# Two attention heads at a time, one per half of TensorE's array and of the partitions

## The chip, the cores and the metric

One core of one Trainium2 chip runs the whole program in one launch. The metric is the device time of an execution in microseconds (us), median over executions. Two rows of the profile with the same name and shape can be passes of one f32 matmul: an f32 matmul is recorded as two.

## The reference

Two transformer blocks at batch 1, 256 tokens (two tiles of 128), width 1024, everything in float32, each block with two layers. In the first block a layer is: a mixer (an LRU, "fox" = causal attention with a forget gate in 8 heads of 64, "ret" = retention in 4 heads of 64), cross attention to a memory (4 heads of 256), and a SwiGLU ffn of 2816. In the second block a layer is: an ffn, a mixer of three branches (NSA with 8 query heads over 2 key heads in a compressed, a selected and a window branch; "sb", stick-breaking attention in 4 heads; "swa", sliding-window attention in 4 query heads over 2 key heads, with sinks), and another ffn. At 256 tokens the selected and the window branch are full causal attention.

```
fox:  softmax(q k^T / 8 + c_q - c_k, causal) v       8 heads
ret:  (q k^T / 8 * decay) v                          4 heads
sb:   w = exp(z - suffix sums of softplus(z)), w v   4 heads
swa:  softmax over 128 keys back, with a sink, v     4 heads
nsa:  g0*compressed + g1*softmax(..)v_slc + g2*softmax(..)v_win   8 heads x 2
```

## The kernel before

**Projections.** All large products run in three passes (high by high, high by low, low by high) with weights that arrive in 1 MB chunks (`Weights._load`, three raw buffers, on SP's queue). ScalarE rounds a chunk's half to the high part (`whi`), VectorE subtracts for the low part (`wlo`); up to six such pieces (`NPIECE`) are ready ahead. One piece of 2 x 512 columns feeds 12 matmuls of 512 columns. `nat_blocks` and `out_rows` loop over pieces and token tiles, with results in two PSUM tiles `acc`.

**Side work.** Attention and norms are Python generators in a list `sides`. After every half of a piece (six matmuls) `pump` steps those generators that are due by a planner (`Pace`): it adds up what each instruction should cost, e.g. on VectorE 0.065 us and 1.045 ns a column, on ScalarE 0.075 us and 0.86 ns a column and 0.09 us for a sum, for a matmul in f32 four passes of its columns at 2.4 GHz, for a DMA its bytes at 360 GB/s and 1.5 us. A generator yields until the planner's time of the data that it needs (`until`). The order so found is fixed in the program; on the chip each engine runs its queue in order. When main work asks for a k tile that isn't made (`need`), the side work is forced. Side work shares two PSUM tiles `aux`; attention's results gather in `o0` and `o1`.

**A head of attention before** (fox `scores`, `softmax_rows`, `transpose_probs`, `pv`; nsa and swa `scores`, `probs`, `turned`, `pv`): q and k lie with the 64 dimensions of two heads on the two halves of the partitions, so a head's score matmuls contract over 64 partitions. The causal 256 x 256 square is 384 columns: 128 for the first token tile, 256 for the second. VectorE adds bias or decay and finds the maximum, ScalarE takes the exponential and its sum. Two heads later the probabilities are turned (three transposes) and copied to SBUF; one head later three matmuls with the turned probabilities stationary and values moving (64 columns) give the result with tokens on partitions. After four heads a group is scaled by the reciprocal sums (and gates), turned with `to_T` (two transposes a token tile) and split into high and low for the next projection. `ret` has no softmax and `sb` two more triangular products; both have the same pattern of scores and `pv`.

**Padding.** `ffn(..., edge)` puts a tile of `edge` bytes a partition ahead of its activations `ahi`, `alo`; `edge` is 960 and 1472 in the first block's layers and 192, 256, 384, 160 in the second's four ffns, in the order in which they run. Tiles of few columns take 32 bytes a partition each in the pool `small`, which lies ahead of these; a tag there has four buffers.

Every engine instruction passes one helper line (150), so rows are told apart by tiles: out<-moving,stationary for a matmul.

Of the kernel before, what the change touches and what calls it, by code (L numbers as in the profile page):

```python
# [154 lines left out]
class Weights:  # L155
# [10 lines left out]
    def plan(self, ap, c0, c1, k0, k1, a_chunk, a_piece, split=True, gain=None):  # L166
        b = c1 - c0
        for k in range(k0, k1, a_chunk):
            a = min(a_chunk, k1 - k)
            ci = len(self.chunks)  # L170
            self.chunks.append((ap[k * P : (k + a) * P, c0:c1].rearrange("(a p) n -> p a n", p=P), a, b))
# [10 lines left out]
    def _load(self):  # L182
        if self.loaded >= len(self.chunks):
            return
        ap, a, b = self.chunks[self.loaded]
        t = self.raw_pool.tile([P, CHUNK], F32, tag="raw", name=f"raw{self.loaded}")
        v = t[:, : a * b].rearrange("p (a n) -> p a n", a=a)
        self.nc.sync.dma_start(v, ap)
        self.raw[self.loaded] = v
        self.loaded += 1  # L190
# [70 lines left out]
def tile_two_blocks(ctx, tc, I, out):  # L261
# [96 lines left out]
    def finish(gen):  # L358
        while any(i[0] is gen for i in sides):
            pump(force=True)  # L360

# [436 lines left out]
    def mixer1(l, T, cos, sin, next_maker):  # L798
        with nc.pool(tc, name=nm("mix1"), bufs=2) as mp:
# [16 lines left out]
            sums = one([P, 2, 8], "sums")  # L816
# [39 lines left out]
            def fox():  # L856
                st, nbs = {}, {}

                def load_nb(h):
                    nb = nbs[h] = mp.tile([P, 384], F32, tag="nb", name=nm("nb"))  # L860
# [4 lines left out]
                def scores(h):  # L865
                    b, r = h // 2, (h % 2) * 64
                    nb = nbs.pop(h)
                    ps = aux()
                    rs = slice(r, r + 64)
                    mm(ps[:, :P], fqT[rs, b, :P], fkT[rs, b, :P], start=True, stop=True)  # L870
                    mm(ps[:, P:384], fqT[rs, b, P:], fkT[rs, b, :], start=True, stop=True)
                    softmax_rows(st, h, ps, nb, sums[:, :, h])

                def softmax_rows(st, h, ps, nb, sum_):
                    sc = mp.tile([P, 384], F32, tag="sc", name=nm("sc"))
                    pr = sc
                    for t, (c0, c1) in enumerate(((0, P), (P, 384))):
                        ngm = sm(1, "ngm")
                        nc.vector.tensor_tensor_reduce(sc[:, c0:c1], ps[:, c0:c1], nb[:, c0:c1], -1.0, 1e38, ALU.add, ALU.min, ngm)
                        nc.scalar.activation(pr[:, c0:c1], sc[:, c0:c1], AF.Exp, bias=ngm, scale=-1.0, accum_out=sum_[:, t : t + 1])  # L880
                    st[h] = pr

                load_nb(0)
                yield
                for i in range(8 + 3):
                    if 0 <= i - 3 < 8:
                        h = i - 3
                        yield from until(st.pop(("T at", h)))
                        if h % 4 == 0:
                            ob = obank()  # L890
                            yield from until(nc.free[ob.tensor.name])
                        pv(ob[:, : 2 * S].rearrange("p (t n) -> p t n", t=2)[:, :, (h % 4) * 64 : (h % 4) * 64 + 64], st.pop(("T", h)),
                           fv[:, :, h * 64 : h * 64 + 64])
                        if h % 4 == 3:
                            g_ = h // 4
                            ri = mp.tile([P, 2, 4], F32, tag="ri", name=nm("ri"))
                            fo = mp.tile([P, 2, S], F32, tag="xs", name=nm("fo"))
                            nc.vector.reciprocal(ri, sums[:, :, 4 * g_ : 4 * g_ + 4])
                            nc.vector.tensor_tensor(fo.rearrange("p t (h d) -> p (t h) d", h=4), ob.rearrange("p (a d) -> p a d", d=64),
                                                    ri.rearrange("p t h -> p (t h)").unsqueeze(2).to_broadcast([P, 8, 64]), op=ALU.mult)  # L900
                            yield True
                            for t in (0, 1):
                                to_T(M, fo[:, t, :], t, 2 + 2 * g_, 2)
                                yield
                    if 0 <= i - 2 < 8:
                        yield from until(st.pop(("at", i - 2)))
                        st[("T", i - 2)] = transpose_probs(mp, st.pop(i - 2))
                        st["T at", i - 2] = nc.end
                        yield
                    if i < 8:  # L910
                        if i < 7:
                            load_nb(i + 1)
                        scores(i)
                        st["at", i] = nc.end
                        yield
# [84 lines left out]
            def ret():  # L1000
# [8 lines left out]
                decays = [load_decay(0)]  # L1009
                st = {}  # L1010
                for i in range(4 + 2):
                    if i < 3:
                        decays.append(load_decay(i + 1))
                    if i >= 2:
                        h = i - 2
                        if h == 0:
# [4 lines left out]
                        yield from until(st.pop(("at", h)))  # L1021
                        pv(ob.rearrange("p (t n) -> p t n", t=2)[:, :, h * 64 : h * 64 + 64], st.pop(h), rvg[:, :, h * 64 : h * 64 + 64])
                    if i < 4:
                        b, r = i // 2, (i % 2) * 64
                        rs = slice(r, r + 64)
                        ps = aux()

                        mm(ps[:, :P], rqkT[rs, 2 + b, :P], rqkT[rs, b, :P], start=True, stop=True)
                        mm(ps[:, P : 2 * P], rqkT[rs, 2 + b, P:], rqkT[rs, b, P:], start=True, stop=True)
                        mm(ps[:, 2 * P : 3 * P], rqkT[rs, 2 + b, :P], rqkT[rs, b, P:], start=True, stop=True)  # L1030
                        w = rot[:, i % 2, : 3 * P].rearrange("p (a q) -> p a q", a=3)
                        decay = decays.pop(0)
                        nc.vector.tensor_tensor(w[:, 0:2, :], ps[:, : 2 * P].rearrange("p (a q) -> p a q", a=2),
                                                decay[:, :P].unsqueeze(1).to_broadcast([P, 2, P]), op=ALU.mult)
                        nc.vector.tensor_tensor(w[:, 2, :], ps[:, 2 * P : 3 * P], decay[:, P:], op=ALU.mult)
                        st[i] = (w[:, 0, :], w[:, 2, :], w[:, 1, :])
                        st["at", i] = nc.end
# [40 lines left out]

    def transpose_probs(pool, pr):

        ps = aux()
        for c in range(3):
            turn(ps[:, c * P : (c + 1) * P], pr[:, c * P : (c + 1) * P], ident)
        w = pool.tile([P, 3, P], F32, tag="pt", name=nm("pt"))
        nc.scalar.copy(w, ps[:, :384].rearrange("p (c q) -> p c q", c=3))
        return (w[:, 0, :], w[:, 1, :], w[:, 2, :])
# [234 lines left out]
    def plan_mixer2(l):  # L1321
        w = I["w_in_2"][l]
        nat = lambda c0, n: W.plan(w, c0, c0 + n, 0, 8, 4 if n > 256 else 8, 2 if n > 256 else 4)
        up = lambda n, k: W.plan(I[f"w_up_{n}_2"][l], 0, D, 0, k, 2, 1)
# [13 lines left out]
        up("swa", 2)  # L1338
        gates(0)
        up("nsa", 4)  # L1340
        W.plan(I["w_out_2"][l], 0, D, 0, 8, 2, 1)

    def mixer2(l, T, next_maker):
        with nc.pool(tc, name=nm("mix2"), bufs=2) as mp:
# [11 lines left out]
            def tanh(out_, in_):  # L1356
# [3 lines left out]
            t2 = lambda: mp.tile([P, 512], F32, tag="t2", name=nm("t2"), bufs=2)  # L1360
            r3 = {"n": lambda: mp.tile([P, 384], F32, tag="rn", name=nm("rn"), bufs=5),
                  "s": lambda: mp.tile([P, 384], F32, tag="rs", name=nm("rs"), bufs=6)}
# [30 lines left out]

            def scores(q, k, rs):
                ps = aux()
                mm(ps[:, :P], q[rs, :P], k[rs, :P], start=True, stop=True)
                mm(ps[:, P:384], q[rs, P:], k[rs, :], start=True, stop=True)
                return ps

            def turned(ring, pr):  # L1400
                ps = aux()
                for c in range(3):
                    turn(ps[:, c * P : (c + 1) * P], pr[:, c * P : (c + 1) * P], ident)
                w = r3[ring]()
                nc.scalar.copy(w, ps[:, :384])
                return w[:, :P], w[:, P : 2 * P], w[:, 2 * P :]
# [20 lines left out]
            def swa():  # L1427
# [21 lines left out]
                ngm, sums = mp.tile([P, 8], F32, tag="wng", name=nm("wng")), mp.tile([P, 8], F32, tag="wsm", name=nm("wsm"))  # L1449
                bias = [load_bias(8), load_bias(9)]  # L1450
                st = {}
                for i in range(4 + 3):
# [15 lines left out]
                    if i < 4:  # L1468
                        if i < 2:
                            bias.append(load_bias(10 + i))  # L1470
# [550 lines left out]
```

## Time and profile before

| | |
|---|---|
| median of 3 executions | 2132.33 us (2129.34 to 2135.59) |
| the profiled execution | 2129.36 us |
| its span in the profile | 2127.4 us |
| TensorE, matmuls | busy 98% of the span |
| weight loads, VectorE, ScalarE, GpSimd | 83%, 59%, 53%, 5% |
| DMA | 179 GB/s over the span |
| granted clock of TensorE | 0.998 of 2.4 GHz |

Busy matmul spans overlap their neighbours, so costs on TensorE are read from one start to the next.

### The profile page before, as it was taken

The numbers are of one execution on the slowest core, as the hardware profiler recorded it, in microseconds if no ns is written. First come the engines' busy times: TensorE is split into PE (matmuls) and PEld (weight loads), VectorE is DVE, ScalarE is ACT, GpSimd is POOL, SyncE is SP. The second block draws the span as 40 slices with busy tenths as digits, with TensorE's granted clock in tenths as the row PEclk, the third lists the DMA queues.
The fourth block names the chain that finished last, engine by engine and source line by source line (L and its number), as shares of the span: only waits on it lengthen the run. The fifth ranks groups of instructions, "written<-read, shape, count | busy, mean of one in ns | idle before, by whom it ended". The sixth has DMA issues, their size and how long they took to land.

```text
span 2127.4 us, 28843 instructions
## 1 busy us (share of the span) xinstructions
PE 2094.0 (98%) x11174; PEld 1763.3 (83%) x11174; DVE 1263.7 (59%) x2079; ACT 1124.5 (53%) x1922; POOL 96.7 (5%) x114
## 2 busy tenths in 40 slices
PE   7999999999999999999999999999999999999999
PEld 6799888888997888788888778888888887778887
DVE  6666565555764655565466556664655556656553
ACT  5456465444565654555355555554555455546552
POOL 0210000001200000000001000000000001000000
PEclk9999999999999999999999999999999999999999
DMA  7456565655465556555546534555555446435553
GB/s 240 156 188 211 172 206 179 217 164 164 155 235 168 198 178 208 178 179 188 198 129 205 164 122 172 196 178 182 177 198 188 161 150 209 163 121 188 178 197 99
DMA packets 204488, 380.88 MB, mean 179 GB/s; under 512 B 14064, under 2 KB 78368, under 8 KB 204352
## 3 DMA queue, kind: packets, MB, share of 16 engines
q1 hardware_dynamic: 192832, 366.46, 52.0%
q10 hardware_dynamic: 11520, 12.59, 1.9%
q8 instruction: 88, 1.44, 0.3%
q14 instruction: 48, 0.39, 0.1%
HBM read 372.03 MB, written 6.99 MB: 178 GB/s over the span
## 4 chain that ended last, share of the span: by engine, by line
PE 87%; DVE 5%; ACT 2%; DMA 2%; issue 2%; SPq 0%; ACTq 0%; POOL 0%; DVEq 0%
PE acc L150 76%; PE aux L150 8%; PE o L150 3%; DVE wlo L150 2%; ACT whi L150 1%; DMA raw<-in_w_in_dram 1%; ACT thi L150 0%; DMA bt<-btiles 0%; DVE t L150 0%; DVE h L150 0%; DMA mem<-in_mem_dram 0%; DVE x L150 0%; DMA hk<-ud 0%; SPq L150 0%; ACT cpr L150 0%
## 5 line engine op out<-in xcount | busy, mean ns | idle before, releaser
L150 PE MATMUL acc<-whi,thi 128*128 128x512 f32 (+2 forms) x1856 | 717.9, 387 | 0.9 <-ACT thi L150 0.5
L150 PE MATMUL acc<-wlo,thi 128*128 128x512 f32 (+2 forms) x1856 | 698.4, 376 | 3.6 <-DVE wlo L150 3.3
L150 PE MATMUL acc<-whi,tlo 128*128 128x512 f32 (+2 forms) x1856 | 699.5, 377 | 2.4 <-DVE tlo L150 2.3
L150 DVE TENSOR_TENSOR wlo<-raw,whi 128x1024 fp32r<-128x1024 f32 (+1 forms) x386 | 467.0, 1221 | 326.9 <-ACT whi L150 325.2
L150 ACT CAST whi<-raw 128x1024 fp32r<-128x1024 f32 (+1 forms) x386 | 394.6, 1037 | 225.1 <-PE acc L150 214.0
L150 DVE SCALAR_TENSOR_TENSOR wlo<-raw,prm,whi 128x512 fp32r<-128x512 f32 (+1 forms) x640 | 398.3, 680 | 174.0 <-ACT whi L150 173.8
L150 ACT ACTIVATE whi<-raw,prm 128x512 fp32r<-128x512 f32 (+1 forms) x640 | 379.9, 663 | 90.5 <-PE acc L150 87.0
L150 PEld LDWEIGHTS acc<-whi,thi 128*128 128x128 f32 x1856 | 350.0, 189 | 71.2 <-issue 11.2
L150 PEld LDWEIGHTS acc<-whi,tlo 128*128 128x128 f32 x1856 | 349.5, 188 | 69.9 <-DVE tlo L150 5.8
L150 PEld LDWEIGHTS acc<-wlo,thi 128*128 128x128 f32 x1856 | 350.3, 189 | 63.6 <-DVE wlo L150 6.6
L150 PE MATMUL acc<-whi,ahi 128*128 128x512 f32 x528 | 208.5, 395 | 0.0
L150 PE MATMUL acc<-whi,alo 128*128 128x512 f32 x528 | 207.2, 392 | 0.0
L150 PE MATMUL acc<-wlo,ahi 128*128 128x512 f32 x528 | 207.2, 392 | 0.0
L150 PEld LDWEIGHTS acc<-whi,alo 128*128 128x128 f32 x528 | 99.1, 188 | 22.2
L150 PEld LDWEIGHTS acc<-wlo,ahi 128*128 128x128 f32 x528 | 99.2, 188 | 21.6
L150 PEld LDWEIGHTS acc<-whi,ahi 128*128 128x128 f32 x528 | 99.2, 188 | 21.4
L150 POOL TENSOR_TENSOR r<-v,mhalf 128x1 f32<-128x1 f32 (+3 forms) x46 | 48.2, 1048 | 1490.8 <-DVE v L150 1490.8
L150 PE MATMUL acc<-thi,whi 128*128 128x256 f32 x384 | 113.2, 295 | 0.0
L150 PE MATMUL acc<-tlo,whi 128*128 128x256 f32 x384 | 109.5, 285 | 0.0
L150 PE MATMUL acc<-thi,wlo 128*128 128x256 f32 x384 | 109.4, 285 | 0.0
L150 DVE SCALAR_TENSOR_TENSOR silu<-acc,r,silu 128x512 f32<-128x512 f32 (+1 forms) x72 | 47.5, 702 | 100.3 <-PE acc L150 100.3
L150 ACT CAST ahi<-aux 128x512 fp32r<-128x512 f32 (+1 forms) x72 | 39.8, 553 | 121.9 <-PE aux L150 121.7
(307 smaller groups left out, 2061.3 us busy)
## 6 DMA issues: line engine op xcount, KB each, us to landing
raw<-in_w_in_dram SPq DMA_DIRECT2D x65, 1024.0 KB, 5.0
raw<-in_ffn_w_gate_dram SPq DMA_DIRECT2D x44, 1024.0 KB, 5.0
raw<-in_ffn_w_up_dram SPq DMA_DIRECT2D x44, 1024.0 KB, 5.0
raw<-in_ffn_w_down_dram SPq DMA_DIRECT2D x44, 1024.0 KB, 4.9
raw<-in_w_gate_dram SPq DMA_DIRECT2D x22, 1024.0 KB, 5.1
raw<-in_w_up_dram SPq DMA_DIRECT2D x22, 1024.0 KB, 5.0
raw<-in_w_down_dram SPq DMA_DIRECT2D x22, 1024.0 KB, 5.1
raw<-in_w_out_dram SPq DMA_DIRECT2D x16, 1024.0 KB, 5.0
```

What stands on the lines that cost most here:

```text
L150: return f(*args, **kwargs)
```

## The change

Heads are taken in pairs in fox, ret, sb, swa and nsa, by one loop `pairs`. Score matmuls of the pair alternate between the halves of the partitions and go to two `aux` tiles. Probabilities are scaled by reciprocal sums (and gates) before the transposes. Values are stationary (64 columns) and turned probabilities move; head 0 lands on partitions 0 to 63 of the result, head 1 on 64 to 127, so that results are already transposed and are split directly (`put_T`); ret keeps `pv`. For grouped heads the pair is one head of either group, so the rows of two up-projection weights are loaded in another order (`halves`). In nsa the compressed branch accumulates into the same result. The ffn pads are 960 in the first block and 128 in the second.

```diff
+    def two_aux():
+        while max([nc.idle(a) for a in auxs[-2:]], default=0.0) > nc.products + 0.3:
+            yield max(nc.idle(a) for a in auxs[-2:])
+
+    def pairs(n, scores, rows, turned, out):
+        at = {}
+        for i in range(n + 2):
+            if 1 <= i <= n:
+                yield from until(at.pop(("scores", i - 1)))
+                if rows:
+                    rows(i - 1)
+                    at["rows"] = nc.end
+                    yield
+            if i >= 2:
+                yield from until(at.pop(("turned", i - 2)))
+                yield from out(i - 2)
+            if 1 <= i <= n:
+                if rows:
+                    yield from until(at.pop("rows"))
+                yield from two_aux()
+                turned(i - 1)
+                at["turned", i - 1] = nc.end
+                yield
+            if i < n:
+                yield from two_aux()
+                scores(i)
+                at["scores", i] = nc.end
+                yield
+
+    HALF = (slice(0, 64), slice(64, P))
+
+    def pair_scores(q, k):
+        pss = aux(), aux()
+        for c, qs, ks in ((slice(0, P), slice(0, P), slice(0, P)), (slice(P, 384), slice(P, S), slice(0, S))):
+            for u in (0, 1):
+                mm(pss[u][:, c], q[HALF[u], qs], k[HALF[u], ks], start=True, stop=True)
+        return pss
...
+    def pair_scale(ws, c):
+        for u in (0, 1):
+            for t, (c0, c1) in enumerate(((0, P), (P, 384))):
+                nc.vector.tensor_scalar(ws[u][:, c0:c1], ws[u][:, c0:c1], c[:, 2 * u + t : 2 * u + t + 1], None, op0=ALU.mult)
+
+    def pair_turn(ws, mk):
+        pss, out_ = (aux(), aux()), []
+        for u in (0, 1):
+            for c in range(3):
+                turn(pss[u][:, c * P : (c + 1) * P], ws[u][:, c * P : (c + 1) * P], ident)
+        for u in (0, 1):
+            w = mk()
+            nc.scalar.copy(w, pss[u][:, :384])
+            out_.append(w)
+        return out_
+
+    def pair_pv(dst, ws, vs, start=True, stop=True):
+        for kt, (c0, c1, q0) in enumerate(((0, S, 0), (S, 384, P))):
+            for u in (0, 1):
+                mm(dst[HALF[u], q0:S], vs[u][:, kt, :], ws[u][:, c0:c1], start=start and kt == 0, stop=stop and kt == 1)
+
+    def put_T(T, kt0, ob):
+        put(T.hi[:, kt0 : kt0 + 2, :], T.lo[:, kt0 : kt0 + 2, :], ob.rearrange("p (c q) -> p c q", c=2))
...
             def fox():
+                def scores(b):
+                    if b:
+                        load_nb(2 * b + 1)
+                    pss = pair_scores(fqT[:, b, :], fkT[:, b, :])
+                    sums[b] = sm(4, "fsum")
...
+                    if b < 3:
+                        load_nb(2 * b + 2)
+
+                def rows(b):
+                    ri = sm(4, "fri")
+                    nc.vector.reciprocal(ri, sums.pop(b))
+                    pair_scale(sc[b], ri)
...
+                yield from pairs(4, scores, rows, turned, out_)
-                            nc.vector.tensor_tensor(fo.rearrange("p t (h d) -> p (t h) d", h=4), ob.rearrange("p (a d) -> p a d", d=64),
-                                                    ri.rearrange("p t h -> p (t h)").unsqueeze(2).to_broadcast([P, 8, 64]), op=ALU.mult)
-                            yield True
-                            for t in (0, 1):
-                                to_T(M, fo[:, t, :], t, 2 + 2 * g_, 2)
...
             def nsa():
+                units = [(rp, b, r) for rp in (0, 1) for b in (0, 1) for r in (2 * rp, 2 * rp + 1)]
+                    pair_pv(dst(r), pt.pop(i), [vsw[:, b, :, g * 64 : (g + 1) * 64] for g in (0, 1)], i % 4 == 0, False)
+                    if i % 4 == 3:
...
+                        for r in (2 * rp, 2 * rp + 1):
+                            mm(dst(r), hold["vbd"][:, r * P : (r + 1) * P], hold["pcT"], start=False, stop=r % 2 == 1)
+                        put_T(Y, 2 * rp, ob[0])
+                yield from pairs(n, scores_, rows, turned_, out_)
...
-        up("swa", 2)
+        up("swa", 2, 2)
-        up("nsa", 4)
+        up("nsa", 4, 4)
...
-            cur = ffn(cur, maker(i), units["next", l], 960 + 512 * l)
+            cur = ffn(cur, maker(i), units["next", l], 960)
-                cur = ffn(cur, maker(i), 0, 128 + {"ffn10": 64, "ffn20": 128, "ffn11": 256, "ffn21": 32}[f"{ph}{l}"])
+                cur = ffn(cur, maker(i), 0, 128)
```

The tags of small tiles `fsum`, `fri`, `wsm`, `wes`, `wng`, `nsum` and `nngm` are new in the pool `small`; `e8` goes.

## Rows read from the trace of the kernel before

**Rows 1.** Page, part 1: busy time of each engine, share of the span, instructions.
```profile
PE 2094.0 (98%) x11174; PEld 1763.3 (83%) x11174; DVE 1263.7 (59%) x2079; ACT 1124.5 (53%) x1922; POOL 96.7 (5%) x114
```
**Rows 2.** Page, part 4: the chain that ended last, by engine.
```profile
PE 87%; DVE 5%; ACT 2%; DMA 2%; issue 2%; SPq 0%; ACTq 0%; POOL 0%; DVEq 0%
```
**Rows 3.** Windows: a stretch in which nsa and swa run in layer 0.
```profile
core 0: us, PE busy (x) PEld busy (x) DVE busy (x) ACT busy (x) POOL busy (x), PEclk, DMA share, GB/s
1160.00:1230.00 70.00, 69.22 (x384) 53.93 (x383) 40.84 (x102) 37.67 (x89) 0.80 (x2) 1.00 0.53 169
```
**Rows 4.** Timeline of TensorE (start, length, instruction): one head's scores in swa.
```profile
1186.39 0.39 PE L150 MATMUL acc<-whi,tlo 128*128 128x512 f32 x1
1186.71 0.92 PE L150 MATMUL aux<-wkT,wqT 64*128 64x128 f32 x4
1187.56 0.50 PE L150 MATMUL acc<-whi,thi 128*128 128x512 f32 x1
1187.90 0.39 PE L150 MATMUL acc<-wlo,thi 128*128 128x512 f32 x1
```
**Rows 5.** Timeline of TensorE: scores of fox's heads 0 and 1, layer 0.
```profile
60.27 0.28 PE L150 MATMUL acc<-thi,wlo 128*128 128x256 f32 x1
60.48 0.93 PE L150 MATMUL aux<-fkT,fqT 64*128 64x128 f32 x8
61.34 0.38 PE L150 MATMUL acc<-thi,whi 128*128 128x256 f32 x1
61.56 0.28 PE L150 MATMUL acc<-tlo,whi 128*128 128x256 f32 x1
```
**Rows 6.** Groups by tile and form on TensorE: busy us, mean ns, idle before.
```profile
L150 PE MATMUL o<-vsw,rn 128*128 128x64 f32 x192 | 25.3, 268 | 0.0
...
L150 PE MATMUL aux<-kT,qT 64*128 64x256 f32 x64 | 19.0, 377 | 0.0
...
L150 PE MATMUL aux<-ident,fo 128*128 128x128 f32 x16 | 2.9, 272 | 0.0
```
**Rows 7.** Timeline of TensorE: one nsa head's values, another's transposes.
```profile
1189.06 0.78 PE L150 MATMUL o<-vsw,rn 128*128 128x64 f32 x6
1189.67 0.50 PE L150 MATMUL aux<-ident,rn 128*128 128x128 f32 x3
1189.92 0.48 PE L150 MATMUL acc<-whi,thi 128*128 128x512 f32 x1
1190.24 0.40 PE L150 MATMUL acc<-wlo,thi 128*128 128x512 f32 x1
```
**Rows 8.** Timeline of TensorE: the cumulative sum, 8 columns stationary, 256 and 128 moving.
```profile
55.02 0.28 PE L150 MATMUL acc<-thi,wlo 128*128 128x256 f32 x1
55.23 0.82 PE L150 MATMUL aux<-ntri,fgt 128*8 128x256 f32 x4
55.98 0.39 PE L150 MATMUL acc<-thi,whi 128*128 128x256 f32 x1
56.20 0.28 PE L150 MATMUL acc<-tlo,whi 128*128 128x256 f32 x1
```
**Rows 9.** Chain in order of time (start, length): two down projections, pads 1472 and 192.
```profile
818.46 55.82 PE acc L150 x246
...
1008.57 57.40 PE acc L150 x246
```
**Rows 10.** Groups by tile and form on VectorE and ScalarE.
```profile
L150 DVE TENSOR_SCALAR cpr<-cpr,cri 128x256 f32<-128x256 f32 x16 | 4.9, 350 | 0.3
L150 ACT ACTIVATE rn<-rn,ngm 128x256 f32<-128x256 f32 x32 | 15.8, 494 | 0.0
L150 ACT ACTIVATION_READ_ACCUMULATOR rn<-rn,ngm 128x1 f32 x64 | 12.0, 187 | 0.0
```
**Rows 11.** DMA issues: count, KB each, median us to landing.
```profile
raw<-in_w_up_nsa_dram SPq DMA_DIRECT2D x4, 1024.0 KB, 5.2
...
nb<-cdram ACTq DMA_DIRECT2D x16, 128.0 KB, 3.7
```
**Rows 12.** Timeline of TensorE: fox's first transposes, with idle time and its end.
```profile
69.80 0.30 PE L150 MATMUL aux<-ident,sc 128*128 128x128 f32 x1 [2.45 <-DVE ngm L150]
```

More of the change, by code (lines that the diff above doesn't have):

```diff
@@ L170, in plan @@
             ci = len(self.chunks)
[L171 removed]
+            if halves:
+                parts = [(slice(64 * g, 64 * g + 64), v[g][:, k : k + a, c0:c1]) for g in (0, 1)]
+            else:
+                parts = [(slice(0, P), ap[k * P : (k + a) * P, c0:c1].rearrange("(a p) n -> p a n", p=P))]
+            self.chunks.append((parts, a, b))
             for j in range(0, a, a_piece):
@@ new lines, in tile_two_blocks, with pair_scores_T @@
+    HALF = (slice(0, 64), slice(64, P))
[5 more added lines that the diff above has]
+        return pss
+    def pair_scores_T(q, k):
+        pss = aux(), aux()
+        for c, ks, qs in ((slice(0, S), slice(0, P), slice(0, S)), (slice(S, 384), slice(P, S), slice(P, S))):
+            for u in (0, 1):
+                mm(pss[u][:, c], k[HALF[u], ks], q[HALF[u], qs], start=True, stop=True)
+        return pss
@@ L883, in fox @@
                 load_nb(0)
+                load_nb(1)
                 yield
[L885 to L898, printed above, removed]
-                            nc.vector.tensor_tensor(fo.rearrange("p t (h d) -> p (t h) d", h=4), ob.rearrange("p (a d) -> p a d", d=64),
-                                                    ri.rearrange("p t h -> p (t h)").unsqueeze(2).to_broadcast([P, 8, 64]), op=ALU.mult)
-                            yield True
-                            for t in (0, 1):
-                                to_T(M, fo[:, t, :], t, 2 + 2 * g_, 2)
[L904 to L915, printed above, removed]
@@ L1008, in ret @@
                     yield
[L1009 to L1016, printed above, removed]
+                decays = [load_decay(0), load_decay(1)]
+                ws, at = {}, {}
+                for b in range(2 + 1):
+                    if b >= 1:
+                        if b == 1:
                             while "rvg" not in flags:
@@ L1020, in ret @@
                             yield from until(nc.free[ob.tensor.name])
[L1021 to L1037, printed above, removed]
+                        yield from until(at.pop(b - 1))
+                        for u in (0, 1):
+                            h, w = 2 * b - 2 + u, ws.pop(u)
+                            pv(ob.rearrange("p (t n) -> p t n", t=2)[:, :, h * 64 : h * 64 + 64], (w[:, :P], w[:, P:S], w[:, S:384]), rvg[:, :, h * 64 : h * 64 + 64])
+                    if b < 2:
+                        yield from two_aux()
+                        pss = pair_scores_T(rqkT[:, b, :], rqkT[:, 2 + b, :])
+                        for u in (0, 1):
+                            w = ws[u] = rot[:, u, :384]
+                            decay = decays.pop(0)
+                            nc.vector.tensor_tensor(w[:, :S], pss[u][:, :S], decay, op=ALU.mult)
+                            nc.vector.tensor_tensor(w[:, S:], pss[u][:, S:384], decay[:, :P], op=ALU.mult)
+                        at[b] = nc.end
+                        if b == 0:
+                            decays += [load_decay(2), load_decay(3)]
                     yield
@@ L1392, in probs @@
                 return sc
[L1394 to L1406, printed above, removed]
             hold = {}
@@ new lines, in rows, with turned_, out_ @@
+                def rows(r):
+                    e = es.pop(r)
+                    nc.vector.tensor_add(e, e, sums.pop(r))
+                    nc.vector.reciprocal(e, e)
+                    pair_scale(sc[r], e)
+                def turned_(r):
+                    pt[r] = pair_turn(sc.pop(r), r3["s"])
+                def out_(r):
+                    if r == 0:
+                        while "cmp" not in hold:
+                            yield False
+                        ob[0] = obank("o1")
+                        yield from until(nc.free[ob[0].tensor.name])
+                    pair_pv(ob[0][:, r * S : (r + 1) * S], pt.pop(r), [wv[:, :, g * 64 : (g + 1) * 64] for g in (0, 1)])
+                    if r == 1:
+                        put_T(Y, 6, ob[0])
@@ L1491, in sqk_done @@
+                yield from pairs(2, scores, rows, turned_, out_)
             def sqk_done(a):
```

264 lines of the change are left out of this document (99 added, 165 removed).

## The prediction

> **What bounds the kernel now.** I read the page first. TensorE is busy for 98% of the span [rows 1], and the chain that ended last lies on it for 87% [rows 2], so a microsecond less of TensorE's own time is a microsecond off the end, as long as nothing late steps into the place. The side work (attention) is slipped between projection matmuls, so I then read single blocks of it in the timeline: not by how long a matmul is shown as busy (those spans overlap) but by start to start, from the last projection matmul before a block to the second one after it, less two ordinary steps (about 0.23 us for 512 columns, 0.12 us for 256). That prices a block with the losses at both its ends. The stage table comes last: where nsa and swa run, VectorE is busy 40.8 of 70 us and ScalarE 37.7 [rows 3], so both have room, but not a free hand.
>
> **Scores, two heads together.** One head alone costs 1187.90 - 1186.39 - 2 x 0.23 = 1.05 us [rows 4], for 384 columns of f32; about 0.2 us of it is lost on either side, where weights aren't loaded ahead. The trace already has one case of what the change does: in fox's first block of layer 0 the planner put the heads 0 and 1 one behind the other, eight matmuls, four of them on each half of the partitions. They cost 61.56 - 60.27 - 2 x 0.12 = 1.05 us [rows 5]. The second head was free: the halves work at the same time, in f32, with both ends' losses paid once. The counts of such lines give the heads: 32 for nsa (two matmul records each for the 256-column form, 64 in all) [rows 6], and by the like rows of the other tiles 16 fox, 8 swa, 8 sb and 8 ret, 72 in all. As 36 pairs they save 36 x 1.05 = 37.8 us. I take off 1.05 for the pair that exists, and 0.7 for one partly interleaved fox and ret block: **36.0 us**. Lower bound: only the ends' losses saved, 36 x 0.4 = 14; the pair in [rows 5] speaks against it.
>
> **Probabilities times values.** Today a head costs 1189.67 - 1189.06 = 0.61 us for six short passes of 64 columns [rows 7]; 64 heads (32 nsa [rows 6], 16 fox, 8 swa, 8 sb; ret keeps the old form) make 39.0 us. After, values are stationary with 64 columns, 384 probabilities' columns move, and the two heads' results go to different halves of the output partitions. No row of before has two such blocks together. The nearest is one block alone of the same moving size with few stationary columns, the cumulative sum of the forget gates: 56.20 - 55.02 - 2 x 0.12 = 0.94 us [rows 8]. If column halves run together as those of rows did, a pair costs 0.94, 32 pairs 30.1, a saving of **8.9 us**. If one after the other, the four passes of the second head, 55.98 - 55.23 less an end of 0.1 = 0.65 us, come on top: 1.59 x 32 = 50.9, a loss of 11.9. I take the first, because the halves in [rows 5] shared everything but the array, and keep the second for the range. The Trainium skill ("TensorE: Matmul & The Clock Gate", section "Measured speedup vs the span model") has 2.38 times for three column tiles, about as for rows: by it the saving would be the 8.9 as well. No run here shows it yet.
>
> **Transposes.** Probabilities are turned as before, three per head. What disappears is the turning of results: 16 matmuls for fox [rows 6], and by the like rows 16 for sb and swa and 16 for nsa. In a row they cost (1190.24 - 1189.67 - 0.23) / 3 = 0.113 us each [rows 7]: 48 x 0.113 = **5.4 us**. The compressed branch keeps its four passes a group, with the operands swapped: nothing.
>
> **Pads ("realigned").** The six ffn phases' down projections, one long piece of the chain each, show two rates: 55.82 / 246 = 0.227 us a matmul, and 57.40 / 246 = 0.233 [rows 9]. Pads of 960, 1472 and 384 bytes go with the first, 192, 256 and 160 with the second (three phases each). Counted in the program's allocation, the first three put the activations at a multiple of 256 bytes in a partition and the others don't. The change adds seven tags of small tiles (four buffers of 32 bytes each, 896) and removes one (128): everything behind moves by 768 bytes, and with pads of 960 and 128 all six land on such a multiple. Three phases x 264 matmuls x 0.0064 = **5.1 us**. Bounds: nothing, or 5.1 lost if the guess of 256 is wrong.
>
> **What is added.** VectorE scales probabilities before the transposes (56 heads, two instructions each; a 256-column one takes 0.35 us [rows 10], so at most 0.7 a head, 39 us in all) and drops the scalings of results, and twelve evictions of 256 columns a layer become six of 512. TensorE's work covers this; without that cover it would be most of those 39 us. The up-projection weights of swa and nsa come in two half-partition loads, six of 1 MB become twelve; SP's queue holds them, no other engine waits on it, and one lands in 5.2 us [rows 11] while the pieces already converted (up to six, each twelve matmuls of 0.227 = 2.7 us) run. Taken at nothing; if the halves landed late, at most 5.2 each.
>
> **New waits.** This is the unknown term. Before, a head's scores and its transposes are two heads apart; now transposes follow their own pair's softmax with nothing of the same chain between. TensorE's queue is in order: where the planner is early, all projection matmuls behind the transposes stand. The planner charges a 256-column exponential with sum 0.075 + 256 x 0.00086 + 0.09 = 0.39 us; the rows have 0.494 + 0.187 = 0.68 [rows 10]. For the four of a pair (two have 128 columns) the shortfall is about 1.2 us; scaling adds some 0.2. The boundaries where side work may enter are six matmuls apart, 1.4 us, which hides about half of it twice over. So 28 pairs (8 fox, 16 nsa, 4 swa) wait between 0 and 1.4 us each: I take 0.5, **14 us**. Fox also loads its second head's decay row just ahead of its use: the planner charges 1.9 us, it lands in 3.7 [rows 11]; behind it on VectorE stand the piece conversions, which have their lead, and the pair's softmax, which hasn't. Six pairs at 0 to 1.8: I take 1.0, **6 us**.
>
> **Sum.** 2129.4 - 36.0 - 8.9 - 5.4 - 5.1 + 20 = 2094 us on the profiled execution. That one lies 3.0 under the median shown, so 2097 for a median.
>
> **Rivals.**
> *Columns one after the other* (0.15): the mode pays off for rows only. 2094 + 8.9 + 11.9 = 2115, or 2118 for a median. For it: no row shows it overlapped, and both heads' moving data span all 128 partitions. Against it: the pair in [rows 5].
> *The planner is early everywhere* (0.13): waits at their upper bounds, 28 x 1.4 + 6 x 1.8 = 50 us: 2124, 2127 for a median, hardly to be told from before.
> *Slower* (0.07): TensorE stands at each pair's transposes. The trace has one such stop: 2.45 us at 69.80, before fox's first transposes, for a softmax [rows 12]. With it in all 28 pairs, 69 us stand against savings of 55.4: 2143, 2146 for a median. It decides from 55.4 / 28 = 2.0 us a pair on. Against it: where nsa and swa run now, TensorE is busy 69.2 of 70 us [rows 3], transposes included.
> *Eviction becomes the bound* (0.03): scaling and softmax bunch, VectorE's work (40.8 of 70 us [rows 3]) comes near all of a shorter stage, and the 39 us come back in place of the 20 of waits: 2113, 2116. The Trainium skill ("TensorEngine Tiling (Array Packing)", section "PSUM Bottleneck") warns of just this: packing speeds the array and not what empties PSUM. By it the savings of the mixers would be lost in part; the trace has the engines 58% busy there, so I give it little.
>
> **How the numbers follow.** The forecast has 0.62: 2097, with its own range 2077 (no waits) to 2112. About 0.3% (6 us) is what a measurement of this kernel can tell. The range for 8 in 10 runs from 2073 (no waits, a little more saved at the blocks' ends) to 2122, past the columns' rival and short of the waits' upper bound. Faster: the forecast, the columns, eviction, and half of the early planner, 0.87; the same: the other half, 0.06; slower: 0.07.
>
> **What would show it.** Scores of a pair at 1.05 us as in [rows 5], in 36 places; a pair's values block near 0.94 us (near 1.6: columns in turn); no transposes of results; all six down projections at 0.227 us a matmul; idle time of TensorE before transposes of probabilities of some 20 us over 28 pairs, with ScalarE's or VectorE's scaled probabilities as releaser. The prediction is wrong if values blocks take 1.6 us, if those waits pass 1.4 us a pair, or if down projections stay at 0.233.

## The result and the profile after

The changed kernel takes 2110.16 us (median of 4 runs, 2107.61 to 2112.83), the kernel before 2133.05 on the same chip: a ratio of 0.9899, 95% interval 0.9887 to 0.9911, or 22.9 us. The forecast was 2097, with a range of 2073 to 2122. The sign and the range held; the gain is a little under two thirds of the one forecast. The profiled execution is the one of 2107.61 us, the fastest of the four, 13.6 above the sum of 2094.

The page's busy times, of the changed kernel (answers to [rows 1]):

```profile
PE 2053.1 (97%) x10982; PEld 1717.3 (82%) x10982; DVE 1276.0 (61%) x2187; ACT 1120.7 (53%) x1910; POOL 84.7 (4%) x110
```

and its chain by engine ([rows 2]):

```profile
PE 83%; DVE 6%; ACT 4%; DMA 4%; issue 2%; POOL 0%; SPq 0%; ACTq 0%; DVEq 0%; POOLq 0%
```

TensorE has 41 us less work, but its share of the chain fell from 87% to 83%: more of the end is now set by what TensorE waits for. The prices of single blocks, in TensorE's timeline of the changed kernel (start, length, instruction; [rows 4, 5, 7]):

```profile
1229.47 0.39 PE L150 MATMUL acc<-whi,tlo 128*128 128x512 f32 x1
1229.79 0.93 PE L150 MATMUL aux<-kT,qT 64*128 64x128 f32 x8
1230.64 0.50 PE L150 MATMUL acc<-whi,thi 128*128 128x512 f32 x1
1230.98 0.39 PE L150 MATMUL acc<-wlo,thi 128*128 128x512 f32 x1
...
1243.72 0.39 PE L150 MATMUL acc<-whi,tlo 128*128 128x512 f32 x1
1244.04 0.87 PE L150 MATMUL o<-rn,vsw 128*64 128x256 f32 x8
1244.84 0.50 PE L150 MATMUL acc<-whi,thi 128*128 128x512 f32 x1
1245.18 0.40 PE L150 MATMUL acc<-wlo,thi 128*128 128x512 f32 x1
```

A pair's scores cost 1230.98 - 1229.47 - 2 x 0.23 = 1.05 us, as forecast: the price of one head. A pair's values cost 1245.18 - 1243.72 - 2 x 0.23 = 1.00 (0.94 forecast; 1.59 if the column halves took turns). The chain in order of time has the six down projections ([rows 9]):

```profile
385.70 51.74 PE acc L150 x228
...
813.90 55.82 PE acc L150 x246
...
1004.06 55.81 PE acc L150 x246
...
1429.66 55.82 PE acc L150 x246
...
1616.91 55.81 PE acc L150 x246
...
2044.16 57.19 PE acc L150 x252
```

All at 0.227 us a matmul. So every price of a block is near its forecast, and much of the shortfall is elsewhere. It is in two views. TensorE's waits, which are called stops below (who it waited for: us in total, times, longest), of the changed kernel ([rows 12] has the like of before):

```profile
PE aux L150 <- DVE rn L150: 6.0, 4, 2.1
PE aux L150 <- DMA w<-in_nsa_cmp_k_w_dram: 3.8, 2, 2.6
PE aux L150 <- DVE rs L150: 2.9, 2, 1.5
...
PE o L150 <- DVE rvg L150: 2.2, 1, 2.2
PE aux L150 <- DVE sc L150: 2.0, 1, 2.0
...
PE acc L150 <- ACT kvout L150: 1.9, 1, 1.9
PE aux L150 <- DVE rot L150: 1.7, 2, 1.5
```

The kernel before has none of these seven lines at 0.2 us or more. The scaled probabilities of nsa, swa and fox (rn, rs, sc) make 10.9 us in seven stops; the loads of the compressed keys' second weights 3.8; the rest stand for tiles that VectorE (rvg, rot) or ScalarE (kvout) finish late. And the windows at some of those stops, with the granted clock third from the end:

```profile
538.00:545.00 7.00, 6.61 (x30) 6.10 (x31) 3.70 (x10) 2.68 (x3) 0.87 (x2) 0.51 0.25 98
562.00:565.50 3.50, 3.50 (x19) 2.56 (x18) 2.70 (x4) 1.61 (x4) 0.00 (x0) 0.51 0.46 126
1261.80:1265.20 3.40, 3.40 (x14) 2.03 (x14) 0.22 (x1) 0.96 (x2) 0.00 (x0) 0.50 0.00 0
```

TensorE runs at half clock (1.2 GHz) there. Each of these stretches comes right behind a stop of 1.9 to 2.2 us: the one at 538 behind the wait for rvg, the one at 562 behind that for kvout, the one at 1261.8 behind that for rn. The other two, of 3.4 us each, come behind the stops for sc (1.96 at 77.01) and for the second weights (2.58 at 1800.63). In all 20.5 us of the changed kernel lie at the lower level, against 6.8 before (ends of the program not counted).

That number belongs to one execution. The changed kernel's second profile (after_again below) has 37.5 us at the lower level, with fewer stops in its sum. One stop, 2.06 us for rn at the end of layer 1's NSA branch, has no low clock at it in the first profile and 10.2 us of it in the second; the first line is of the changed kernel, the second of after_again:

```profile
1877.00:1884.00 7.00, 6.19 (x28) 3.88 (x29) 1.38 (x4) 2.49 (x4) 0.00 (x0) 1.00 0.00 0
1876.80:1887.00 10.20, 8.99 (x26) 6.00 (x27) 1.85 (x6) 2.49 (x4) 0.00 (x0) 0.50 0.00 0
```

What holds in every execution is the direction: the eight of the changed kernel have a granted clock of 0.991 to 0.996, those of the kernel before that were run beside the experiments 0.997 to 1.000.

Put together from the two traces (TensorE's matmuls start to start; stops of over 60 ns counted apart; a matmul at half clock priced as its like at full clock, the excess in a line of its own; from the first matmul on):

```
us                                    before    after     diff   forecast
projections                           1483.7   1484.3     +0.6        0
down projections                       365.8    361.0     -4.8     -5.1
scores, and small products              94.4     64.1    -30.3    -36.0
values                                  59.3     48.8    -10.5     -8.9
turning                                 87.4     84.9     -2.5     -5.4
stops                                   19.5     39.5    +20.0    +20
excess of matmuls at half clock          3.2      9.9     +6.7        0
sum                                   2113.3   2092.5    -20.8    -35.4
```

One product of the compressed branch changes its line: it stands under "scores, and small products" before (3.0 us) and under "values" after (3.7). By the same working the second profile of the changed kernel has 36.4 us of stops and an excess of 17.1, so these two lines are good to some us only.

### The profile page after: what moved, and what is told of

Its sections match the earlier page's. It is cut to its first block, busy times and chain, and to the rows that moved or that the text cites. A ratio compares the mean times of both kernels' runs of the same rounds, so it can differ in the third digit from the quotient of the medians.

```text
span 2105.8 us, 28507 instructions
## 1 busy us (share of the span) xinstructions
PE 2053.1 (97%) x10982; PEld 1717.3 (82%) x10982; DVE 1276.0 (61%) x2187; ACT 1120.7 (53%) x1910; POOL 84.7 (4%) x110
## 4 chain that ended last, share of the span: by engine, by line
PE 83%; DVE 6%; ACT 4%; DMA 4%; issue 2%; POOL 0%; SPq 0%; ACTq 0%; DVEq 0%; POOLq 0%
PE acc L150 74%; PE aux L150 6%; DVE wlo L150 3%; PE o L150 3%; ACT whi L150 1%; DMA nb<-cdram 1%; DMA raw<-in_w_in_dram 1%; DMA w<-in_nsa_cmp_k_w_dram 1%; ACT rn L150 1%; ACT thi L150 1%; DMA kvd<-kvout 0%; SPq L150 0%; DVE t L150 0%; DVE h L150 0%; DMA mem<-in_mem_dram 0%
```

## The experiments

Ratios are to the kernel before, whose median beside these runs was 2128.5 to 2129.6 us. First the scale of the group: the changed kernel again.

> The changed kernel itself once more, so that the edits of this group stand beside it on the same chip. Every theory expects a ratio to the kernel before of 0.990, within its uncertainty of 0.0012.

Measured 2109.79, ratio 0.9903 (0.9888 to 0.9919).

**The realigned activations.** Undone in the changed kernel (960 and 128 bytes become 960 + 64 and 128 + 64), and done alone in the kernel before:

```diff
-  128 + {"ffn10": 64, "ffn20": 128, "ffn11": 256, "ffn21": 32}[f"{ph}{l}"]
+  128 + 256
```

> The changed kernel with 64 bytes more ahead of the activations in all six feed-forward phases, nothing else. Theory (a down projection whose activations don't begin on a multiple of 256 bytes runs at 0.233 us a matmul in place of 0.227): all six of them become slow, 228 + 4 x 246 + 252 = 1464 matmuls at 0.0064 us more, so 9.4 us slower than the changed kernel's 2110.2, about 2119.6. Rival (the three slow ones of the kernel before were slow for another reason, their place in the program or the data that stands beside them): within 2 us of 2110.2.

> The kernel before with the gaps of its second block all at 384 bytes, so that all six of its feed-forward phases have their activations on a multiple of 256 bytes; no pairs. Theory: its three slow down projections (1008.57, 1442.95 and 2064.28) fall to 0.227 us a matmul, 246 + 246 + 252 = 744 matmuls at 0.0064 us, so 4.8 us faster than before, about 2128.3, and the pairs alone are worth the other 18 of the change's 22.9 us. Rival: no change, within 1.5 us of 2133.

Measured: pads64 2116.63, ratio 0.9946 (0.9933 to 0.9960), 0.0045 above the mean of the changed kernel's two, 9.6 us; before_pads 2124.83, ratio 0.9981 (0.9972 to 0.9991), 4.0 us faster than before. The chain of pads64, then that of before_pads:

```profile
387.51 53.21 PE acc L150 x228
819.01 57.40 PE acc L150 x246
```

```profile
1009.73 55.81 PE acc L150 x246
1442.64 55.82 PE acc L150 x246
```

pads64 has all six at 0.233, before_pads all six at 0.227; the second fence has two of the three that were slow before ([rows 9] has one). Nothing but the address of what lies behind the pad differs, so the address is the cause, and some 18 of the 22.9 us are the pairs' own. That the step is 256 bytes rests on the four offsets seen, worked from the pads' sizes and the prediction's count that a pad of 384 was in place before: 0 runs at 0.227, and 32, 64 and 128 (pads 160, 192 and 256 before) at 0.233. Other offsets were not tried.

**The order of the halves.** The loop over the halves goes outside that over the columns; scores and values alike:

```diff
-  for c, qs, ks in (...):
-      for u in (0, 1):
+  for u in (0, 1):
+      for c, qs, ks in (...):
           mm(pss[u][:, c], q[HALF[u], qs], k[HALF[u], ks], start=True, stop=True)
```

> The changed kernel with the matmuls of a pair in another order: both of the first half, then both of the second, where the changed kernel alternates between the halves. Same instructions. Theory (two halves run side by side only as neighbours in the queue): of 384 columns a head only the middle ones overlap, 640 columns' worth a pair in place of 384, so a pair's scores take 1.6 to 2.0 us in place of 1.05 and its products with the values 1.2 in place of 1.00; 36 pairs and 32 pairs make 25 to 40 us at most, less what the stops of the changed kernel give back: 2125 to 2145. Rival (what a pair costs doesn't hang on the order): 1.05 us a pair, 2110.

Measured 2104.13, ratio 0.9881 (0.9862 to 0.9900): not slower. TensorE's timeline of u_outer:

```profile
1231.06 0.39 PE L150 MATMUL acc<-whi,tlo 128*128 128x512 f32 x1
1231.38 0.93 PE L150 MATMUL aux<-kT,qT 64*128 64x128 f32 x8
1232.24 0.50 PE L150 MATMUL acc<-whi,thi 128*128 128x512 f32 x1
1232.58 0.39 PE L150 MATMUL acc<-wlo,thi 128*128 128x512 f32 x1
```

1232.58 - 1231.06 - 0.46 = 1.06 us, where 1.6 or more was expected. My theory fell: the halves run side by side without being neighbours in the kernel's text. The prediction's own [rows 5] had spoken against it: fox's heads 0 and 1 stand there one behind the other, and cost 1.05 us. In the single records of this block the 128-column matmuls of both halves come first, 14 ns apart (13 in most of u_outer's blocks, and in the block of [rows 5]), then those of 256 columns, though the kernel's text has the first half's 256-column matmul between them; in the alternating order of the changed kernel the first two start 6 or 7 ns apart. The trace doesn't list the order of the queue itself.

**The scaling.** It is left out:

```diff
 def pair_scale(ws, c):
-    for u in (0, 1):
+    for u in ():
```

> The changed kernel without the scaling of the probabilities by their row sums (28 pairs, 4 multiplications each, 1.01 us on VectorE a pair), so its attention isn't normalised. Theory (the scaling moved from the narrow results to the wide probabilities, and stands on VectorE between the exponentials and the turning): the NSA branch ends sooner, its last block falls from 13.1 us to 9 or less, VectorE has 28 us less to do, and time falls by 6 to 14 us, to 2096 to 2104. Rival (gaps between projection blocks set the pace, whatever stands in them): within 3 us of 2110.

Measured 2098.80, ratio 0.9843 (0.9822 to 0.9864), 11 to 13 us under the changed kernel: the theory's side. The end of the NSA branch in TensorE's timeline, first of the changed kernel, then of no_scale:

```profile
1253.62 0.39 PE L150 MATMUL acc<-whi,tlo 128*128 128x512 f32 x1
1253.94 0.87 PE L150 MATMUL o<-rn,vsw 128*64 128x256 f32 x8
1255.79 1.16 PE L150 MATMUL aux<-ident,rn 128*128 128x128 f32 x6 [0.98 <-DVE rn L150]
1257.06 1.43 PE L150 MATMUL aux<-kT,qT 64*128 64x128 f32 x8
1258.42 0.87 PE L150 MATMUL o<-rn,vsw 128*64 128x256 f32 x8
1261.35 1.44 PE L150 MATMUL aux<-ident,rn 128*128 128x128 f32 x6 [2.06 <-DVE rn L150]
1262.73 2.24 PE L150 MATMUL o<-rn,vsw 128*64 128x256 f32 x8
1264.89 1.27 PE L150 MATMUL o<-bc,kk 128*128 128x256 f32 x4
1266.84 0.50 PE L150 MATMUL acc<-whi,thi 128*128 128x512 f32 x1 [0.68 <-ACT thi L150]
1267.18 0.40 PE L150 MATMUL acc<-wlo,thi 128*128 128x512 f32 x1
```

```profile
1253.21 0.39 PE L150 MATMUL acc<-whi,tlo 128*128 128x512 f32 x1
...
1256.73 0.87 PE L150 MATMUL o<-rn,vsw 128*64 128x256 f32 x8
1257.56 0.33 PE L150 MATMUL aux<-ident,rn 128*128 128x128 f32 x1
1258.05 0.71 PE L150 MATMUL aux<-ident,rn 128*128 128x128 f32 x3 [0.16 <-ACT rn L150]
...
1262.93 0.40 PE L150 MATMUL acc<-wlo,thi 128*128 128x512 f32 x1
```

In the changed kernel the projection has run out: the last pairs' steps follow one another with nothing between, and TensorE stands twice for scaled rows, its clock falling behind the second. Without the scaling the same block takes 1262.93 - 1253.21 - 0.46 = 9.3 us in place of 1267.18 - 1253.62 - 0.46 = 13.1. But the stops of the whole kernel are 35.7 us, where the changed kernel's two profiles have 39.5 and 36.4; others came up (1.9 us twice for the merging of the branches on VectorE). The clearer difference is in the clock: 13.7 us at the lower level against 20.5 and 37.5, an excess of 5.9 against 9.9 and 17.1. And with less work on VectorE the planner orders the steps otherwise, so the run prices the scaling's work and place together, not apart.

**Loads.**

```diff
 def scores(b):
-    if b:
-        load_nb(2 * b + 1)
...
     if b < 3:
         load_nb(2 * b + 2)
+        load_nb(2 * b + 3)
```

and the first two decay tiles, the second weights and masks likewise ahead.

> The changed kernel with loads issued earlier and nothing else moved: the forgetting gate's rows of a pair of FoX heads right behind the scores of the pair before, the first two decay tiles of the retention before its turning, the second weights and masks of the compressed keys at the start of the NSA branch. Theory (a pair asks for two loads where a head asked for one, and they come just in time): the stops of the changed kernel between 530 and 534 (1.70 us) and those for the second weights (1.26 at 1186.56, 2.58 at 1800.63) go, and with them some of the 20 us at half clock: 5 to 12 us faster, 2098 to 2105 against 2110. Rival (each of these stops is followed by another that is nearly as late): the loads no longer end the waits, and time stays within 3 us.

Measured 2105.60, ratio 0.9880 (0.9864 to 0.9897): 4 to 5 us under the changed kernel, with intervals that just overlap. The lines for the second weights (3.8 us) and rot (1.7) are gone from TensorE's waits; the one for rvg grew from 2.2 to 3.2, one of 2.3 us for thr (ScalarE) came up, and the last block of the first NSA branch took 14.3 us in place of 13.1. Time at half clock is 27.3 us, between the 20.5 and 37.5 of the changed kernel's two profiles. Of 5.5 us of stops, 1.8 are gone from the sum of all, and none against the second profile of the changed kernel.

**The order of the NSA branch.** Six runs move its steps, alone or with the early loads. merge issues the rows' scaling in the gap of the next step (in fox and swa too, which use the same loop); skew issues scores a pair ahead, with two gaps a pair; nsa_first lets the branch go first where several are ready; skew2_loads groups the steps of two gaps otherwise and has the early loads; combo is skew2_loads with nsa_first, loads_first the early loads with nsa_first. skew, skew2_loads and combo also take six row buffers in place of five and fewer buffers of four small tiles; their down projections stay at 0.227 us a matmul.

```diff
 # merge
     rows(i - 1)
     at["rows"] = nc.end
-    yield
 # nsa_first
-    step(due[0])
+    step(min(due, key=lambda i: not i[3]))
...
-                side(nsa())
+                side(nsa(), True)
 # skew
+    def pairs_ahead(n, scores, rows, turned, out):
...
+            if i < n:
+                yield from two_aux()
+                scores(i)
...
+            if 1 <= i <= n:
+                yield from until(at.pop(("scores", i - 1)))
+                rows(i - 1)
...
+                yield from out(i - 2)
...
+                turned(i - 1)
```

> The changed kernel, but in the loop over pairs the scaling of the rows and the product with the values of the pair before it are issued in the same gap between two projection blocks, so three gaps a pair in place of four. Theory (the loss is in the number of gaps: a pair of the NSA branch takes about 10 us for four of them, where two heads took 6.8 us before, and the branch is late for its projection): a pair falls to about 8 us, the stop at the end of each NSA branch (13.1 us for one block at 1253.9) falls by some 5 us and time by 5 to 12 us, to 2098 to 2105. Rival (the loss is in loads that come late, and the gaps don't matter): within 3 us of 2110.

Measured 2107.38, ratio 0.9907 (0.9894 to 0.9920): the rival's side. With three gaps in place of four the last block still takes 12.8 us, and a stop of 2.94 us for the merging of the branches comes up at 1217.28.

> The changed kernel, but the NSA branch issues the scores of a pair ahead of the turning of the pair before it, so that the exponentials of one pair run while the other is turned and multiplied: two gaps a pair. Six row buffers in place of five. Theory (gaps and a serial step): a pair takes 5 to 7 us, the branch ends ahead of its projection as in the kernel before, the stops of both layers (13.1 us for one block at 1253.9, where its matmuls need about 5) and the half-clock stretches behind them go: 10 to 20 us faster than the changed kernel, 2090 to 2100. Rival (late loads): within 3 us of 2110. A second rival (VectorE and ScalarE are the bound of that branch): a pair stays at 9 us or more, though two gaps hold it.

Measured 2112.12, ratio 0.9927 (0.9915 to 0.9940): no gain, if anything a loss. The last block fell as expected, from 13.1 to 7.6 us (it holds 32 matmuls in place of 48), but inside the branch there is a new stop (TensorE's timeline of skew):

```profile
1214.13 0.39 PE L150 MATMUL acc<-whi,tlo 128*128 128x512 f32 x1
1217.97 0.50 PE L150 MATMUL acc<-whi,thi 128*128 128x512 f32 x1 [3.46 <-DVE merged L150]
```

A projection waits for its accumulators, which VectorE empties (merged) only after the compressed keys' softmax and this branch's eviction, now bunched ahead of it, and after 1.97 us in which VectorE itself stands for ScalarE's whi, which comes behind the exponentials of rn.

> The changed kernel, but where several branches have a step ready between two projection blocks, the NSA branch goes first; the steps and their work are the same. Theory (the NSA branch is a chain of its own that begins at 1158 and takes 108 us, its first three pairs 17 to 23 us each because the window branch and the compressed keys take turns with it for the two score banks; the projection waits for its end): the first pairs come down to 12 us, the block at the end of the branch falls from 13.1 us to 2, and if nothing else takes its place, time falls by 6 to 14 us. What may take its place: the window branch, which the projection asks for earlier, then shows a block of its own of over 8 us, and time stays within 4 us. Rival (the stops come from VectorE and ScalarE being full, whatever the order): no block shrinks.

Measured 2105.93, ratio 0.9888 (0.9874 to 0.9902). The stops at the branch's end are gone, but there is now one block of 16.6 us from 1211.5 on, with swa's steps in it and no projection, 10.2 us of it at half clock. What was said to take the place took it.

> The changed kernel with the early loads of the run loads_early, and in the NSA branch two gaps a pair: the scores of a pair together with the scaling of the pair before, then the product with the values and the turning; scores ahead of the turning of the pair before. Theory (the chain of the NSA branch is what the projection waits for): the last block falls from 14.5 us (loads_early) to 7 or less and time by 6 to 14 us against loads_early's 2105.6, to 2092 to 2100. Rival (a stop that is taken away at the end of the branch comes back inside it, as in skew, where 3.5 us appeared at 1218 on VectorE's merging): within 3 us of 2105.6.

Measured 2107.25, ratio 0.9899 (0.9886 to 0.9912): the last block is down to 5.8 us, as the theory said, and the time is not; the rival's side.

> The changed kernel with the early loads, the two gaps a pair in the NSA branch, and the NSA branch first. Theory: the projection no longer waits at the branch's end at all (some 20 us of projections stand behind its last product), so both layers gain 5 to 8 us each: 2088 to 2098. Rival: the window branch is now the late one (its steps are issued in one block without a projection between, which cost 10 us or more), and time stays at 2100 to 2108.

Measured 2113.70, ratio 0.9928 (0.9916 to 0.9940), slower than the changed kernel's 0.9899 and 0.9903, with intervals that touch at most; the rival went further than I put it. In TensorE's timeline of combo, TensorE stands 5.00 us for the compressed branch's probabilities, in a block of 19.5 us without a projection:

```profile
1216.57 0.87 PE L150 MATMUL o<-rs,wv 128*64 128x256 f32 x8
1222.45 1.07 PE L150 MATMUL aux<-ident,pc 128*128 128x128 f32 x2 [5.00 <-DVE pc L150]
```

> The two edits that helped most alone, together: early loads (2105.6) and the NSA branch first (2105.9), against 2109.8 for the changed kernel on the same scale. If they take different waits away (the loads those in FoX and before the second weights, the order those at the end of the NSA branch), they add: 2101 to 2103, a ratio of 0.986 to 0.987. Rival (the block of the window branch in the middle of the second mixer, 16.7 us in nsa_first, sets the time of that mixer, and an earlier load only makes it begin earlier): 2104 to 2107, as each alone.

Measured 2107.81, ratio 0.9905 (0.9888 to 0.9921): the two edits don't add.

Over the changed kernel and all its rearrangements (stops of over 0.12 us from the program's start: 47.2 us changed, 48.3 merge, 48.9 skew, 45.4 loads_early, 42.9 nsa_first, 48.0 skew2_loads, 53.6 combo, 45.6 loads_first; 28.6 in the kernel before) the sum stays between 42.9 and 53.6; the changed kernel's own second profile has 45.5. A stop taken away in one place turns up in another. None of them beats the changed kernel by more than the uncertainty of both. loads_early comes nearest (0.9880), and u_outer, which moves no step, is as near (0.9881): gains of this size can't be put down to the steps.

## Why the prediction was right, and where it was off

- **Scores, 1.05 us a pair:** right as a price: 23 pairs that stand alone between projections cost 1.04 to 1.06 us, two of swa 1.20. The total was too high. Start to start, the scores' own matmuls fell by 27.3 us where 36.0 was forecast; the other 3.0 of the table's line is the compressed branch's product that left it. I charged every head the price of a block alone, ends included. Before, 45 of the 70 gaps with scores held other work too, and the projections at the ends, where part of that price was booked, did not get cheaper (+0.6). How much of the difference that is, no run settles.
- **Values:** the column halves run together, in 1.00 us against 0.94; the rival "columns one after the other" (1.59) falls. The heads' own products fell from 40.5 to 26.2 us, 14.3 for 8.9: the forecast had set a pair's price with its ends against a head's without them (0.61). Scores and values together gave 41.6 for 44.9, so most of the two errors may be one of where the ends are booked.
- **Transposes of results:** gone, as the counts show, and worth 4.9 us for 5.4. But "Probabilities are turned as before" was wrong: in the same number of matmuls those of rn went from 10.7 to 12.2 us (11.6 in the second profile) and those of rs from 2.5 to 3.3, so turning as a whole fell by 2.5. Why, no run shows.
- **Pads:** 4.8 us in the rows, 5.1 forecast; both single runs bear out the address.
- **New waits:** the size was right (+20.0 for +20, +16.9 in the second profile) and the picture wrong, so that the sums agree is luck. Not 0.5 us at each of 28 pairs and 1.0 at each of six loads, but 13 stops of 0.9 to 2.6 us; seven of them, 10.9 us, for scaled probabilities, the rest at loads and evictions I had put at nothing or elsewhere (the second weights, rvg, kvout). Over 28 pairs the seven are 0.4 us a pair, inside the bound of 1.4 that the prediction had set for itself; four single pairs pass it (1.5 to 2.1).
- **What was off: the step "New waits" has no term for the clock.** It counts the time for which TensorE stands, and not the matmuls at half clock that come behind some of the stops. 20.5 us run at 1.2 GHz where it was 6.8, and their excess is 6.7 us that no term of the sum held. It is the largest piece of the 14.6 us between the two sums (by the table's lines: 6.7 clock, 5.7 scores, 2.9 turning, 0.6 projections, 0.3 pads, less 1.6 values). In the second profile it would be 13.9. That the stops cause the low clock is argued from what stands ahead of it; no run takes the stops away and leaves the rest.
- **"TensorE's work covers this", of the scaling:** too kind. In the stretch of [rows 3] VectorE went from 40.84 to 50.05 of 70 us and TensorE from 69.22 to 66.73, as this window of the changed kernel shows:

```profile
1160.00:1230.00 70.00, 66.73 (x365) 50.56 (x365) 50.05 (x129) 38.48 (x85) 0.80 (x2) 1.00 0.59 166
```

  no_scale puts the scaling, by its work and its place, at some 11 us. Its rival ("eviction becomes the bound", 2113 to 2116) got the mechanism in part: VectorE isn't full, but on the chain where projections run out. The Trainium skill ("TensorEngine Tiling (Array Packing)", section "PSUM Bottleneck") says that packing speeds TensorE and not what empties PSUM; here the trace agrees in part: 10.9 us of stops are for VectorE's work behind the scores, but for scaling in SBUF and not for emptying PSUM; an accumulator that VectorE hasn't emptied stops TensorE in skew (3.46 us).
- **Why rearranging doesn't help** is shown only as far as the sum goes: a stop moves. One reason that fits but was not tried: a pair takes both score tiles `aux` at once, so the branches have to take turns for them. A third score tile would tell.

## What to carry to other kernels

Pairing heads gives the second head's scores for nothing (1.05 us for one head and for two) and makes the products with values about a third shorter (40.5 to 26.2 us, start to start); it makes the turning of probabilities and the other steps behind the scores no shorter: cost the chain from scores through softmax and scaling to turning as well, and look at where the projections that should cover it run out. Where results land transposed, the scaling moves from the narrow result to the wide probabilities, ahead of the turning; that is a term of its own. When pricing a stop of TensorE of about 2 us, look in the trace for whether the clock falls behind one, and add it, from more than one execution: here one kernel had 20.5 and 37.5 us at half clock.

## What the hardware showed that I had not expected

- Matmuls on different halves of the array start in another order than the kernel's text: with all of one half's matmuls ahead of the other's, a pair still costs 1.06 us, and the halves' first matmuls start 13 to 14 ns apart. The Trainium skill ("TensorE: Matmul & The Clock Gate", section "The mechanism") has matmuls start strictly in the order of the program; the trace of u_outer differs, as far as the kernel's text gives the order of the queue, and the measurement decides.
- Two f32 column halves (64 columns stationary each, 256 and 128 moving) cost 1.00 us for two heads, where one block alone of the same moving size cost 0.94 [rows 8]; with one half's matmuls ahead of the other's it is 1.01.
- 64 bytes of address are worth 0.0064 us for each matmul of 512 columns: 0.227 us at a multiple of 256 bytes, 0.233 beside it, in six phases each way.
- In the changed kernel's first profile five stops of 1.9 to 2.6 us have 3.4 to 6.8 us at 1.2 GHz behind them, and two of the same length (1.92 at 40.37, 2.06 at 1877.02) have none. The second of these two has 10.2 us at 1.2 GHz in the second profile.
